# Decoder step on one core: u blocks split only where they are used, candidate sums by segments, three PSUM banks for u, and a set order of gate and u evictions

## The chip, the core and the metric

The kernel runs on one core of one Trainium2 chip. The metric is the device time of one execution in microseconds (us): the median of the runs. A change of 0.2% is about 6 us here.

## The reference, cut to what matters

One inference step of two layers, for 512 prompt tokens and 8 samples (520 tokens, padded to five tiles of 128 in places). Layer 0 mixes with gated DeltaNet and RG-LRU, layer 1 with sliding-window attention. After each mixer comes PEER, a lookup among 16384 experts:

```python
q = (tb @ w_q).reshape(PEER_BLOCK, PEER_HEADS, 2, PEER_D_SUB)
s = jnp.einsum('thcd,hcnd->thcn', q, sub_keys).astype(F32)
s_top, i_top = lax.top_k(s, PEER_TOPK)
cand = (s_top[:, :, 0, :, None] + s_top[:, :, 1, None, :]).reshape(PEER_BLOCK, PEER_HEADS, -1)
cand_idx = (i_top[:, :, 0, :, None] * PEER_N_KEYS + i_top[:, :, 1, None, :]).reshape(...)
best, pos = lax.top_k(cand, PEER_TOPK)
expert = jnp.take_along_axis(cand_idx, pos, axis=-1)
gate = jax.nn.softmax(best, axis=-1)
act = jax.nn.gelu(jnp.einsum('td,thkd->thk', tb, u_tab[expert]).astype(F32))
return jnp.einsum('thk,thkd->td', (gate * act).astype(tb.dtype), v_tab[expert])
```

## The kernel before, in words

Products of float32 operands are made of float16 halves: `split` copies a float32 tile to float16 on ACT (hi) and takes the rest on DVE (lo), and `mm3` issues three matmuls (hi with hi, hi with lo, lo with hi).

Each layer is a mixer and then `peer(layer)`. For the first 384 prompt tokens PEER is dense: the activations of all 16384 experts are computed in 128 **u blocks** of 128 experts. A u block is one load of 512 KB from `uT`, a split (`wh` on ACT, `wl` on DVE, pools of two buffers each), 24 matmuls of 384 columns into one PSUM bank (`pu`), and a gelu on ACT (`act`, L333) that reads the bank and so frees it. For the last 128 prompt tokens and the samples the experts are gathered row by row instead: POOL issues indirect DMAs (`row`, L357), DVE takes dot products with the token (L364) for u, and scaled sums (L545) for v.

The stages of `peer` are these.

- **Queries**: 16 blocks of `wq` on PE; on DVE the top 16 of each half for all tiles (`topk_half`, tiles `scs` and `swork`).
- **Pairs**: `topk_pairs` for the samples, for two halves of the gathered tile (`pairs3`) and for tile 0 (`pairs`). It adds up the candidate pairs (`cand`, L256, 16 instructions a call, one for each rank a of the first half) and their expert numbers (`ce`, L260, 33 instructions a call), takes the top 16 of 50 candidates and finds their numbers by comparisons (`eq`). Six calls are made in a layer. Meanwhile PE works on u blocks, and the gathered dot products run on DVE.
- **Gates**: for each of 3 tiles 4 parts of 32 tokens, `gates(t, part, us)`. DVE makes one-hot tiles (`oh`), PE multiplies them into `pg` (four banks), ACT copies each `pg` to `stage` (8 copies of 128x512 a part), and one DMA on ACT's queue writes the 2 MB of `stage` to `GD` in DRAM. `stage` has one buffer: the first copy of a part waits for the write of the part before. `run_u` issues u blocks between the copies.
- **Main**: for each of the 128 blocks the activations are multiplied by the gates read back, and `yps` accumulates the products with v. The u blocks that are left run here beside it. `peer` computes 79 blocks ahead of the main loop in program order, and 49 in it.

Of the PSUM's eight banks the pairs and gates stages hold two for `pu`, two for `pt` and four for `pg`.

**Blocks of u split beforehand.** At the end of each mixer `presplit` loads blocks of `uT` by halves (`pst`), splits each half in two pieces (`ppr`, on ACT and DVE), and writes the halves in float16 to DRAM (`PW`, 256 KB a write). `NPRE = (16, 12)`: 16 blocks for layer 0, 12 for layer 1. `ublock` then loads such a block (`wpr`, 512 KB) ready for PE, where any other is loaded in float32 and split.

**What sets the order.** The program is recorded, and a list scheduler that runs a timeline of its own puts the instructions of each engine in an order, across stages; on the chip each engine and each DMA queue takes them in that order. So `presplit`, written last in the mixer, is put between the mixer's own instructions, and blocks of u between those of pairs and gates.

## Time and profile before

| | us |
|---|---|
| median of 3 runs (lowest, highest) | 3012.0 (3011.1, 3014.87) |
| the profiled execution, its own time | 3010.68 |
| its span, first to last instruction | 3008.9 |
| outside the span | 1.8 |
| mean granted TensorE clock | 0.983 of 2.4 GHz |

How to read the profile: PE is TensorE's matmuls, PEld its weight loads, DVE VectorE, ACT ScalarE, POOL GpSimd, SP the engine that issues most DMAs. Times are in us from the start of the span. The view of stretches gives each engine's busy time in it, with the number of instructions in brackets, the granted clock, the busy share of the DMA engines and GB/s. The view of waits names the waiting engine and line, what released it, the total, the number of waits and the longest. Matmuls overlap in the records (one of 384 columns is shown with some 328 ns, and the next starts half of that later), so that a busy PE can still be a slow one; the number of matmuls in a stretch says how fast it went.

In this execution layer 0's mixer lies before 380, its queries end on DVE at 492, its pairs reach to 634 (the first one-hot tile), its gates to 886 (the first `yps`), its main stage to 1575. In layer 1 the same marks are 1780, 1906, 2057, 2317 and the end.

### The profile page before, as it was taken

How to read it: one execution, taken by the hardware profiler on the slowest of the kernel's cores; microseconds unless marked ns; L12 is line 12 of the kernel's file. 1: busy time of each engine (PE TensorE's matmuls, PEld its weight loads, DVE VectorE, ACT ScalarE, POOL GpSimd, SP SyncE). 2: the span in 40 equal slices, each digit the busy share in tenths (PEclk: the TensorE clock that was granted, in tenths of full speed). 3: DMA queues.
4: the chain of work that ended last, by engine and by line, in shares of the span. 5: the costliest groups of instructions: out<-in, count | busy, mean ns of one | idle time of the engine just before them, and what ended most of it. 6: DMA issues, size and time to landing. Idle time of an engine off the chain costs nothing.

```text
span 3008.9 us, 49598 instructions
## 1 busy us (share of the span) xinstructions
PE 2845.8 (95%) x18198; PEld 1726.9 (57%) x18198; DVE 2569.4 (85%) x5871; ACT 1319.3 (44%) x2171; POOL 856.1 (28%) x662
## 2 busy tenths in 40 slices
PE   8979999899999999999998899989999999999998
PEld 7768586456655555544446559645665555554443
DVE  6756789999978988889995879989987898898998
ACT  4743332356753333333335743335765333333342
POOL 2300101310024555435520000130002555454552
PEclk9999999999999999999999999999999999999999
DMA  4264424866699999999977422686569999999996
GB/s 136 72 218 149 147 86 161 295 238 217 217 339 390 366 354 363 363 358 370 352 276 246 154 79 85 211 293 213 193 216 327 390 360 360 353 359 359 362 357 234
DMA packets 332104, 798.78 MB, mean 265 GB/s; under 512 B 28611, under 2 KB 165259, under 8 KB 328020
## 3 DMA queue, kind: packets, MB, share of 16 engines
q1 hardware_dynamic: 241004, 442.78, 43.5%
q0 software_dynamic: 78336, 285.25, 25.5%
q10 hardware_dynamic: 12520, 67.58, 6.1%
q8 instruction: 142, 2.33, 0.3%
q14 instruction: 102, 0.84, 0.1%
HBM read 700.96 MB, written 93.17 MB: 264 GB/s over the span
## 4 chain that ended last, share of the span: by engine, by line
PE 66%; DVE 13%; DMA 10%; ACT 6%; issue 4%; POOL 1%; SPq 0%; ACTq 0%; DVEq 0%; POOLq 0%
PE yps L607 30%; PE pu L88 7%; PE pu L86 7%; PE pu L87 7%; DMA row<-in_u_rows,elist 2%; ACT stage L72 2%; PE pq L87 2%; DMA GD<-stage 2%; PE pq L86 2%; PE pq L88 2%; DVE wl L81 2%; DMA pst<-in_uT 2%; DVE row L364 1%; DMA PW<-ppr 1%; DMA gl<-GD 1%
## 5 line engine op out<-in xcount | busy, mean ns | idle before, releaser
L607 PE MATMUL yps<-vv,vw 128*128 128x512 f16 x4536 | 1010.8, 379 | 10.3 <-ACT vv L72 8.1
L607 PEld LDWEIGHTS <-vw 128*128 128x128 f16 x4608 | 450.4, 98 | 542.2 <-issue 17.0
L357 POOL DMA_INDIRECT row<-in_v_rows,elist x272 | 395.4, 1454 | 862.9 <-issue 251.0
L88 PE MATMUL pu<-xh,wl 128*128 128x384 f16 x1824 | 598.4, 329 | 34.2 <-DVE wl L81 33.7
L86 PE MATMUL pu<-xh,wh 128*128 128x384 f16 x1824 | 598.9, 328 | 15.6 <-ACT act L333 10.7
L87 PE MATMUL pu<-xl,wh 128*128 128x384 f16 x1824 | 598.4, 328 | 0.0
L357 POOL DMA_INDIRECT row<-in_u_rows,elist x272 | 389.1, 1430 | 679.8 <-DVE best L237 250.3
L72 ACT ACTIVATE wh<-wst 128x1024 f16<-128x1024 f32 x296 | 312.4, 1056 | 565.3 <-PE pu L87 340.3
L81 DVE SCALAR_TENSOR_TENSOR wl<-wst,wh 128x1024 f16<-128x1024 f32 x296 | 361.7, 1223 | 154.1 <-ACT wh L72 148.1
L88 PEld LDWEIGHTS <-wl 128*128 128x128 f16 x2912 | 287.4, 99 | 186.9 <-DVE wl L81 47.5
L86 PEld LDWEIGHTS <-wh 128*128 128x128 f16 x2912 | 290.1, 100 | 159.3 <-ACT wh L72 25.5
L87 PEld LDWEIGHTS <-wh 128*128 128x128 f16 x2912 | 287.6, 99 | 149.3 <-issue 14.5
L72 ACT ACTIVATE vv<-row 128x1024 f16<-128x1024 f32 x252 | 263.1, 1048 | 232.9 <-PE yps L607 182.6
L81 DVE SCALAR_TENSOR_TENSOR vv<-row,vv 128x1024 f16<-128x1024 f32 x252 | 307.6, 1221 | 49.9 <-ACT vv L72 48.1
L545 DVE SCALAR_TENSOR_TENSOR yac<-row,wgt,yac 128x1024 f32<-128x1024 f32 x268 | 343.5, 1282 | 4.5 <-DMA row<-in_v_rows,elist 2.6
L364 DVE CUSTOM_DVE_ANT_0 row<-row,xtok 128x1024 f32<-128x1024 f32 x256 | 308.4, 1220 | 20.3 <-DMA row<-in_u_rows,elist 20.1
L72 ACT ACTIVATE vw<-act 128x384 f16<-128x384 f32 x256 | 129.7, 516 | 350.8 <-PE yps L607 298.1
L72 ACT ACTIVATE stage<-pg 128x512 f32<-128x512 f32 x192 | 183.4, 1105 | 76.2 <-DMA GD<-stage 65.6
L79 DVE TENSOR_TENSOR vw<-act,vw 128x384 f16<-128x384 f32 x256 | 139.8, 553 | 24.3 <-ACT vw L72 23.6
L333 ACT ACTIVATE act<-pu 128x384 f32<-128x384 f32 x256 | 122.3, 478 | 48.4 <-PE pu L88 46.2
L87 PE MATMUL pq<-xl,wh 128*128 128x264 f16 (+1 forms) x480 | 132.9, 277 | 0.5 <-DVE xl L79 0.3
L88 PE MATMUL pq<-xh,wl 128*128 128x264 f16 (+1 forms) x480 | 132.9, 277 | 0.0
(501 smaller groups left out, 3968.4 us busy)
## 6 DMA issues: line engine op xcount, KB each, us to landing
row<-in_v_rows SPq DMA_DIRECT2D x256, 512.0 KB, 7.8
wst<-in_uT SPq DMA_DIRECT2D x228, 512.0 KB, 6.3
GD<-stage ACTq DMA_DIRECT2D x24, 2048.0 KB, 7.6
gl<-GD SPq DMA_DIRECT2D x64, 768.0 KB, 7.9
wst<-in_wq SPq DMA_DIRECT2D x32, 512.0 KB, 3.4
pst<-in_uT SPq DMA_DIRECT2D x56, 256.0 KB, 4.1
PW<-ppr SPq DMA_DIRECT2D x56, 256.0 KB, 2.9
wpr<-PW SPq DMA_DIRECT2D x28, 512.0 KB, 5.2
```

Of the source, the lines that this page charges most:

```text
L72: self.nc.scalar.activation(out, in_, AF.Copy, scale=scale)
L79: eng.tensor_sub(lo, src, hi)
L81: eng.scalar_tensor_tensor(lo, src, scale, hi, op0=OP.mult, op1=OP.subtract)
L86: mm(out, wh, xh, start=start, stop=False)
L87: mm(out, wh, xl, start=False, stop=False)
L88: mm(out, wl, xh, start=False, stop=stop)
L333: S.activation(t, ps[:, 0:ND], AF.Gelu_apprx_tanh, scale=1.0 / SCW)
L357: G.indirect_dma_start(out=r, out_offset=None, in_=src, in_offset=bass.IndirectOffsetOnAxis(ap=elist[:, k:k + 1], axis=0))
L364: V.tensor_tensor_reduce(u, u, self.xtok[:, 0] if k < P else xrep, 1.0, 0.0, OP.mult, OP.add, hd[:, k:k + 1])
L545: V.scalar_tensor_tensor(dst, vbuf.pop(n), wgt[:, k:k + 1], dst, op0=OP.mult, op1=OP.add)
L607: T.matmul(yps[t][:, o], w[:, a, c], v[:, b, o], start=x == 0 and k == 0, stop=x == P - 1 and k == 2)
```

## The change

1. `NPRE` is (0, 0): `presplit` does nothing, and every block of u is loaded in float32 and split in `peer`.
2. The sums of candidates are written by segments. Ranks that take the same range of the second half are added in one instruction with two broadcast operands: 7 instructions in place of 16 for `cand` (`CSEG`), 20 in place of 33 for `ce` (`LSEG`, whose runs of equal ranges are joined). The candidates and their order stay.
3. In the pairs and gates stages `pt` keeps one bank in place of two; the freed bank goes to `pu`, so that every third u block (u % 3 == 2) has a bank of its own pool (`third`). This holds from the first pairs to the end of the gates; ahead of them and behind them there are two banks as before.
4. In `gates` two of its three u blocks are recorded ahead of the part, the third at its middle; and the first copy to `stage` of a part is ordered on ACT behind the last ACT instruction recorded before it, the gelu of the second block (`last_on`, `behind`: an edge of order on the engine, with no semaphore).

```diff
--- before.py
+++ after.py
@@ -43,13 +43,18 @@
         for a in range(hi):
             b0, b1 = (hi - 4) // (a + 1), hi // (a + 1)
             if b1 > b0:
-                seg.append((a, b0, b1))
+                if seg and seg[-1][1:] == (a, b0, b1):
+                    seg[-1] = (seg[-1][0], a + 1, b0, b1)
+                else:
+                    seg.append((a, a + 1, b0, b1))
                 perm += [start[a] + b for b in range(b0, b1)]
         cnt.append(len(perm))
     return seg, cnt, np.array(perm, np.float32)
 
 
 LSEG, LCNT, LPERM = lookup_order()
+
+CSEG = [(a0, a1, 0, TOPK // a1) for a0, a1 in ((0, 1), (1, 2), (2, 3), (3, 4), (4, 5), (5, 8), (8, 16))]
 SCW = 1024.0
 SCV = 256.0
 SCG = 64.0
@@ -108,6 +113,18 @@
                 for q in range(0, 4, 2):
                     self.split(o[:, 0, q:q + 2], o[:, 1, q:q + 2], st[:, q:q + 2], SCW)
                 nc.sync.dma_start(self.PW[layer, b, :, :, c], o)
+
+    def behind(self, ins):
+
+        ctx = ExitStack()
+        for i in ins:
+            ctx.enter_context(self.tc.issue_after(i))
+        return ctx
+
+    def last_on(self, *engines):
+
+        ins = self.nc.cur_bb.bb.instructions
+        return [next(i for i in reversed(ins) if i.engine == e.engine) for e in engines]
 
     def ublock(self, layer, b):
         if b < self.NPRE[layer]:
@@ -250,16 +267,18 @@
         V.tensor_scalar(fx[:n, 0], fx[:n, 0], float(P), None, op0=OP.mult)
         cand = pool.tile([P, HM, NC50], F32, name="cand%d" % HM)[:, 0:H]
         ce = pool.tile([P, HM, NC50], F32, name="ce%d" % HM)[:, 0:H]
-        off = 0
-        for a in range(TOPK):
-            nb = TOPK // (a + 1)
-            V.tensor_add(cand[:n, :, off:off + nb], st[:, 0, :, a:a + 1].to_broadcast([n, H, nb]), st[:, 1, :, 0:nb])
-            off += nb
-        off = 0
-        for a, b0, b1 in LSEG:
-            V.tensor_add(ce[:n, :, off:off + b1 - b0], fx[:n, 0, :, a:a + 1].to_broadcast([n, H, b1 - b0]),
-                         fx[:n, 1, :, b0:b1])
-            off += b1 - b0
+
+        def sums(out, x, segs):
+
+            off = 0
+            for a0, a1, b0, b1 in segs:
+                s = [n, H, a1 - a0, b1 - b0]
+                o = out[:n, :, off:off + s[2] * s[3]].rearrange("p h (a b) -> p h a b", a=s[2])
+                V.tensor_add(o, x[:n, 0, :, a0:a1, None].to_broadcast(s), x[:n, 1, :, None, b0:b1].to_broadcast(s))
+                off += s[2] * s[3]
+
+        sums(cand, st, CSEG)
+        sums(ce, fx, LSEG)
         best = pool.tile([P, HM, TOPK], F32, name="best%d" % HM)[:, 0:H]
         pos = pool.tile([P, HM, TOPK], U32, name="pos%d" % HM)[:, 0:H]
         wk = pool.tile([P, NC50], F32, name="cwork")
@@ -312,6 +331,7 @@
 
         act, upair = {}, {}
         nprep, nu, live = [0], [0], [0]
+        third = []
 
         def u_prep():
             if nprep[0] < P:
@@ -324,7 +344,7 @@
                 return
             nu[0] += 1
             h, l = upair.pop(u)
-            ps = pu.tile([P, 512], F32, name="pu")
+            ps = (third[0] if third and u % 3 == 2 else pu).tile([P, 512], F32, name="pu")
             for kb in range(KB):
                 self.mm3(ps[:, 0:ND], h[:, kb], l[:, kb], self.xh[:, kb, 0:ND], self.xl[:, kb, 0:ND],
                          kb == 0, kb == KB - 1)
@@ -433,8 +453,9 @@
         TG = 32
         with tc.tile_pool(name="gates", bufs=1, reuse_waits="tile") as gp, \
                 tc.tile_pool(name="pairs", bufs=1, side="right", reuse_waits="tile") as tp, \
-                tc.tile_pool(name="topkps", bufs=2, space=bass.MemoryType.PSUM, reuse_waits="tile") as psum:
+                tc.tile_pool(name="topkps", bufs=1, space=bass.MemoryType.PSUM, reuse_waits="tile") as psum:
             lts = {}
+            third.append(psum)
 
             def pairs3(h0):
 
@@ -473,6 +494,8 @@
 
                 lt = lts[t]
                 stage = gp.tile([P, P, TG], F32, name="stage")
+                run_u(us - 1)
+                order = self.last_on(S)
                 for t4 in range(0, TG, 4):
                     if t4 % 8 == 0:
 
@@ -492,8 +515,10 @@
                         q, r = divmod(t4 % 8 + k, 2)
                         T.matmul(pg[:, k], oh[:, 0, q, :, r], oh[:, 2, q, :, r], start=True, stop=False)
                         T.matmul(pg[:, k], oh[:, 0, q, :, r], oh[:, 3, q, :, r], start=False, stop=True)
-                    self.copy(stage[:, :, t4:t4 + 4].rearrange("p i t -> p t i"), pg)
-                    if t4 * us // TG < (t4 + 4) * us // TG:
+                    with self.behind(order):
+                        self.copy(stage[:, :, t4:t4 + 4].rearrange("p i t -> p t i"), pg)
+                    order = []
+                    if t4 == TG // 2:
                         run_u(1)
                 nc.scalar.dma_start(GD[P // TG * t + part], stage)
 
@@ -527,6 +552,7 @@
                     pairs(k // 4 + 1)
                     pairs_t(k // 4 + 1)
             run_u(P)
+        third.clear()
         kctx.close()
 
 
@@ -1528,8 +1554,8 @@
             self.UP = 7
             dp = ctx.enter_context(tc.tile_pool(name="scratch", bufs=1, space=bass.MemoryType.DRAM))
             self.GD = dp.tile([12, P, P, 32], F32, name="GD")
-            self.NPRE = (16, 12)
-            self.PW = dp.tile([2, max(self.NPRE), P, 2, KB, P], F16, name="PW")
+            self.NPRE = (0, 0)
+            self.PW = dp.tile([2, max(1, *self.NPRE), P, 2, KB, P], F16, name="PW")
             self.AD = dp.tile([self.NSP, P, ND], F32, name="AD")
             self.wst = ctx.enter_context(tc.tile_pool(name="wst", bufs=3))
             self.wsp = ctx.enter_context(tc.tile_pool(name="wsp", bufs=2))
```

What the scheduler makes of it is shown at three places. **ACT, layer 0's mixer**, where the inverse of chunk matrices runs (`ia` to `ie` are its copies out of PSUM, `zth` a tanh of another projection, `ppr` the first half of a presplit). Before:

```order
L72 ACTIVATE ppr<-pst 128x256 x4
L72 ACTIVATE id<-psg_2238 128x512
L1141 ACTIVATE zth<-psp 128x256
L72 ACTIVATE ie<-psg_2252 128x512
L72 ACTIVATE ppr<-pst 128x256 x4
L72 ACTIVATE ia<-psg_2229 128x512
L72 ACTIVATE ppr<-pst 128x256 x2
L72 ACTIVATE ia<-psg_2266 128x512
```

Now, at the same place:

```order
L77 ACTIVATE ia<-psg_2218 128x512
L77 ACTIVATE id<-psg_2238 128x512
L77 ACTIVATE wh<-wst 128x1024
L1167 ACTIVATE zth<-psp 128x256
L77 ACTIVATE ia<-psg_2229 128x512
L77 ACTIVATE ie<-psg_2252 128x512
```

The pieces of `presplit` that stood between the copies of the inverse are gone; nothing was put in their place.

**DVE, layer 0's pairs**, at the last comparisons of the first `pairs3` (`row,hd` is a gathered dot product, `wl` the lower half of a u block). Before:

```order
L279 TENSOR_TENSOR eq_6136<-pf_6122,lperm 128x800
L364 ISA row,hd<-row,xrep 128x1024
L364 ISA hd 128x1
L241 MAX_INDEX pos_6291<-best_6290,cwork 128x8
L281 TENSOR_TENSOR eq_6136<-eq_6136,ce_6046 128x800
L239 MATCH_REPLACE cwork<-best_6290,cand_6239 128x50
L364 ISA row,hd<-row,xrep 128x1024
L364 ISA hd 128x1
L282 TENSOR_REDUCE ev<-eq_6136 128x4x4
```

Now:

```order
L86 SCALAR_TENSOR_TENSOR wl<-wst,wh 128x1024
L384 ISA row,hd<-row,xrep 128x1024
L384 ISA hd 128x1
L298 TENSOR_TENSOR eq_5868<-pf_5854,lperm 128x800
L256 MATCH_REPLACE cwork<-best_6012,cand_5983 128x50
L384 ISA row,hd<-row,xrep 128x1024
L384 ISA hd 128x1
L300 TENSOR_TENSOR eq_5868<-eq_5868,ce_5800 128x800
L86 SCALAR_TENSOR_TENSOR wl<-wst,wh 128x1024
```

Lower halves of u blocks now stand among the pairs from their start, where blocks split beforehand needed none. Between the last `swork` of the queries and the first one-hot tile DVE has 17 of them in layer 0 before and 32 now, and 23 and 33 in layer 1; four more stand ahead of that point, in either layer. Its sums of candidates there go from 196 to 112 instructions, and from 49 to 23 in the gates. PE has 33 whole blocks of u ahead of layer 0's first gate matmul before and 37 now, 35 and 38 in layer 1.

**ACT, layer 1's gates**, one late part, from one write of `GD` to the next. Before:

```order
L498 DMA GD<-stage 128x4096
L72 ACTIVATE wh<-wst 128x1024
L333 ACTIVATE act<-pu 128x384
L72 ACTIVATE stage<-pg 128x4x128 x4
L72 ACTIVATE wh<-wst 128x1024
L333 ACTIVATE act<-pu 128x384
L72 ACTIVATE wh<-wst 128x1024
L333 ACTIVATE act<-pu 128x384
L72 ACTIVATE stage<-pg 128x4x128 x4
L498 DMA GD<-stage 128x4096
```

Now:

```order
L523 DMA GD<-stage 128x4096
L77 ACTIVATE wh<-wst 128x1024
L353 ACTIVATE act<-pu 128x384
L77 ACTIVATE wh<-wst 128x1024
L353 ACTIVATE act<-pu 128x384
L77 ACTIVATE stage<-pg 128x4x128 x4
L77 ACTIVATE wh<-wst 128x1024
L353 ACTIVATE act<-pu 128x384
L77 ACTIVATE stage<-pg 128x4x128 x4
L523 DMA GD<-stage 128x4096
```

Two gelus in place of one stand between a write of `GD` and the copy that waits for it. Layer 0's late parts stood so already before.

## Rows read from the trace of the kernel before

**Rows 1.** The page: each engine's busy time, share of the span, instructions.

```profile
PE 2845.8 (95%) x18198; PEld 1726.9 (57%) x18198; DVE 2569.4 (85%) x5871; ACT 1319.3 (44%) x2171; POOL 856.1 (28%) x662
```

**Rows 2.** Stretches: both mixers where presplits run, then the pairs of both layers.

```profile
core 0: us, PE busy (x) PEld busy (x) DVE busy (x) ACT busy (x) POOL busy (x), PEclk, DMA share, GB/s
160.00:260.00 100.00, 84.02 (x633) 75.96 (x633) 56.88 (x131) 46.73 (x123) 0.66 (x1) 0.89 0.72 227
1600.00:1700.00 100.00, 81.41 (x650) 66.03 (x649) 69.28 (x265) 70.39 (x206) 0.00 (x0) 0.93 0.67 213
...
492.00:634.00 142.00, 123.98 (x725) 71.01 (x724) 127.52 (x553) 44.15 (x66) 49.35 (x38) 0.96 0.85 289
...
1906.00:2057.00 151.00, 131.14 (x760) 75.09 (x758) 136.81 (x572) 49.84 (x72) 50.58 (x38) 0.95 0.84 286
```

**Rows 3.** Waits between 160 and 260, layer 0's mixer.

```profile
DVE ppr L81 <- ACT ppr L72: 31.1, 19, 7.5
ACT ppr L72 <- DMA PW<-ppr: 25.1, 19, 2.9
ACT ppr L72 <- DMA pst<-in_uT: 9.3, 1, 9.3
```

**Rows 4.** Waits between 1600 and 1700, layer 1's mixer.

```profile
ACT ppr L72 <- DMA pst<-in_uT: 20.6, 9, 3.9
DVE ppr L81 <- ACT ppr L72: 16.6, 9, 3.3
```

**Rows 5.** The chain from 160 to 290 by line, as shares of that stretch.

```profile
by line: DMA PW<-ppr 24.4%; PE psg L987 11.4%; DMA pst<-in_uT 6.4%; PE psa L1191 6.1%; DMA S<-in_state_gdn 6.1%; DVE ppr L81 5.4%; ACT ppr L72 5.2%; ACT dT L1011 3.2%; issue 2.6%; PE psa L1007 2.3%; PE psp L987 2.0%; PE psa L1008 1.9%; PE p
```

**Rows 6.** The presplits' own instructions in two stretches: DVE busy, ACT busy, clock, DMA.

```profile
160.00:260.00 100.00, 24.48 (x64) 23.06 (x64) 0.89 0.72 227
1600.00:1700.00 100.00, 17.21 (x44) 15.95 (x44) 0.93 0.67 213
```

**Rows 7.** Stretches of layer 0's mixer ahead of the presplits and behind them.

```profile
100.00:140.00 40.00, 36.31 (x305) 30.72 (x303) 30.71 (x57) 32.48 (x51) 11.30 (x21) 1.00 0.21 67
260.00:300.00 40.00, 39.44 (x273) 31.64 (x271) 24.41 (x49) 13.02 (x23) 0.54 (x1) 0.98 0.29 98
```

**Rows 8.** The u blocks' instructions alone in four stretches: PE, PEld, DVE, ACT.

```profile
500.00:520.00 20.00, 19.84 (x122) 0.00 (x0) 0.00 (x0) 2.57 (x6) 1.00 0.81 269
540.00:640.00 100.00, 83.73 (x483) 0.00 (x0) 0.00 (x0) 9.79 (x21) 0.95 0.89 303
...
634.00:886.00 252.00, 203.15 (x1185) 0.00 (x0) 0.00 (x0) 23.36 (x49) 0.99 0.66 239
2057.00:2317.00 260.00, 202.40 (x1180) 0.00 (x0) 0.00 (x0) 23.58 (x49) 0.99 0.64 227
```

**Rows 9.** Groups of DVE instructions between 492 and 634, busy us and mean ns.

```profile
L81 DVE SCALAR_TENSOR_TENSOR wl<-wst,wh 128x1024 f16<-128x1024 f32 x17 | 20.7, 1215 | 1.4 <-ACT wh L72 1.4
L260 DVE TENSOR_TENSOR ce<-fx 128x8 f32<-128x8 f32 (+5 forms) x132 | 11.2, 167 | 0.0
```

**Rows 10.** DVE in order of time: start, us, instruction.

```profile
524.93 1.53 DVE L260 TENSOR_TENSOR ce<-fx 128x8 f32<-128x8 f32 x19
526.36 0.22 DVE L240 MAX8 best<-cwork 128x8 f32<-128x50 f32 x1
```

**Rows 11.** Waits between 492 and 634, layer 0's pairs.

```profile
PEld L88 <- DVE wl L81: 15.4, 9, 5.7
DVE row L364 <- DMA row<-in_u_rows,elist: 12.4, 8, 2.6
```

**Rows 12.** Waits between 640 and 880, layer 0's gates.

```profile
ACT stage L72 <- DMA GD<-stage: 25.3, 9, 4.3
```

**Rows 13.** Waits between 2080 and 2310, layer 1's gates.

```profile
ACT stage L72 <- DMA GD<-stage: 40.3, 10, 6.4
DVE wl L81 <- ACT wh L72: 32.6, 10, 4.4
```

**Rows 14.** The page: a DMA's KB and median us from issue to landing.

```profile
GD<-stage ACTq DMA_DIRECT2D x24, 2048.0 KB, 7.6
```

**Rows 15.** Waits of the whole span.

```profile
PE pu L86 <- ACT act L333: 15.7, 16, 2.7
```

## The prediction

> **What bounds the kernel now.** I read the page first: PE is busy for 95% of the span [rows 1], so time can come only from the rest, or from stretches in which a busy PE is slow. The view of stretches finds these. In layer 0's mixer from 160 to 260 and in layer 1's from 1600 to 1700, PE is idle for 16.0 and 18.6 us of 100, at a granted clock of 0.89 and 0.93 [rows 2]. In the pairs it is idle for 18.0 us of 142 and 19.9 of 151, and there DVE is busy for 127.5 and 136.8 [rows 2]: DVE sets the pace. At full pace 122 matmuls of u blocks run in 20 us, 3.93 us for a block of 24; from 540 to 640 only 483 run in 100 us, 4.97 us a block [rows 8], and PE's weight loads wait 15.4 us for `wl` [rows 11].
>
> The gates are nearly full: 252 us in layer 0 with 1185 matmuls of u, 49.4 blocks [rows 8]. These take 194 us at 3.93; 768 gate matmuls of a third of the columns take, at a third of 0.164 us, 42 (an estimate). So 16 us are lost, and by the same sum on 1180 matmuls 25 of layer 1's 260 [rows 8]. The main stages I leave out: the change issues nothing there, and the number of u blocks recorded ahead of them stays.
>
> **Presplits out of the mixers.** The waits tell what they do in an engine's order. In layer 0's stretch ACT is busy for 46.7 us and waits 25.1 for writes of `PW` and 9.3 for `pst` [rows 2, 3]: 81 us in which little else passes. DVE is busy for 56.9 and waits 31.1 for ACT's half [rows 2, 3]. The mixer's own copies stand behind these waits, and PE behind the copies. The chain agrees: writes of `PW`, loads of `pst` and both halves of the split make 41.4% of 130 us, 54 us [rows 5]. In layer 1 ACT is busy for 70.4 and waits 20.6, and DVE is busy for 69.3 and waits 16.6 [rows 2, 4]. Without the presplits' own 24.5 and 17.2 us on DVE and 23.1 and 16.0 on ACT [rows 6], both engines have half of each stretch free.
>
> What is late next is PE and the alternation of PE with a copy. The gain can't be the chain's 54 us: PE is busy for 84.0 and 81.4 us anyway [rows 2]. It lies between 0, if the alternation alone makes PE wait, and PE's idle time, 34.6 us together; a clock that recovers could add some. The nearest rows without presplits are the same mixer ahead of them and behind them, where PE is idle for 9% and 1.4% of the time [rows 7]. I take 5%: 84.0/0.95 = 88.4, a gain of 11.6, and 81.4/0.95 = 85.7, a gain of 14.3. **Together -26.** The DMAs go too, 56 loads and 56 writes in the mixers; on SP's queue the loads of states and of output weights no longer stand behind writes that wait for DVE. That is part of the same gain. The 28 loads of `wpr` become 28 loads of `wst` of the same 512 KB, at nothing: three buffers cover them as before.
>
> **The split moves into the pairs, and the sums shrink.** In layer 0's pairs DVE gets 15 more `wl` at 1.22 us [rows 9], 18.3, and one dot product that was counted in the gates, 1.2. It loses 84 of its sums. One is shown with 0.167 us [rows 9], but 19 of them pass in 1.43 us, from 524.93 to 526.36 [rows 10], 0.075 each; since the elements are still added, that is the price of an instruction, 6.3 for 84. DVE's work goes to 127.5 + 13.2 = 140.7. Its idle time, 14.5 us, is mostly the 12.4 of waiting for gathered rows [rows 11], which nothing here changes: I keep it. Four more `wl` less 22 sums stand ahead of the stretch, 4.9 - 1.7 = 3.2. So the first one-hot tile comes 16.4 us later, and PE has done four more u blocks by then, 15.7 us: +0.7 net. In layer 1, 10 more `wl` are 12.2, less 6.3, plus 3.2: 9.1 us later, and three more blocks, 11.8: -2.7. **Together -2.** ACT's 28 copies hide there: it is busy for 44 and 50 us of these stretches [rows 2].
>
> The Trainium skill ("VectorE: DVE Perf Modes", Side-by-side: where the cycles go) adds about 150 cycles of start and decoding to a DVE instruction, 0.16 us at its clock. Here 264 sums fewer (22 in each of 12 calls) would by that be worth 41 us, where 0.075 makes 20; the sum would fall by 21 us. The trace differs: these instructions start 0.075 us apart, so it decides.
>
> **Order in the gates.** A copy to `stage` that waits for the write of `GD` holds back the next `wh` behind it on ACT, then `wl` on DVE, then PE. ACT waits 25.3 us so in layer 0 and 40.3 in layer 1, where DVE waits 32.6 for `wh` [rows 12, 13]. The write lands in 7.6 us [rows 14]; two u blocks take PE 7.9, so with two gelus between, as the order now has in the late parts of both layers, the copy should find it landed. The added edge orders ACT alone and no one waits for it longer than for that second gelu; what is queued behind it, `wh` of the third block, has a block's time. I take 12 us lost a layer in place of 16 and 25: -4 and -13. The ends are 0 and all that is lost, 41. DVE loses 26 sums more in each, hidden where PE is the bound. **Together -17.**
>
> **The third bank.** PE waits 15.7 us for a gelu in the whole span, in 16 waits [rows 15], many of them of blocks that then wait for `wl`. Between 0 and -15.7; I cost it at 0, since DVE holds the pairs and two banks did for the gates of layer 0. `pt`'s lost bank costs nothing: three transposes a tile.
>
> **The sum**: -26 - 2 - 17 = -45, on the profiled execution's 3010.7: 2966. The median of the runs is 1.3 higher, so I forecast **2967**, and 2945 to 2990 with these terms.
>
> **Rivals.**
> - *The mixers are bound by their own alternation.* For it: the matmuls of the inverse wait for a copy of the product before them, and the idle 9% of rows 7 has no presplit. Against it: the chain runs through `PW` [rows 5]. With 5 us in place of 26, or with a gates term of next to nothing: 2985.
> - *Slower: DVE can't feed PE through the pairs.* `wh` and `wl` have two buffers each, so a block that comes late on DVE stops PE at once. Blocks split in the pairs now take 4.97 us in place of 3.93 [rows 8]. If the 28 blocks that came ready now lose 1.04 us each, that is +29; the pairs' late end leaves the gates 6 of their 17, and the mixers give only 10: +13, **3025**. It decides from the point where the pairs lose more than the mixers give. For it: DVE has 90% of these stretches already. Against it: the sums that go, and an order that now spreads `wl` evenly.
> - *A sum is worth its whole duration*, because dependent sums don't overlap as those of rows 10 do. 264 at 0.167 in place of 0.075 [rows 9, 10] make 24 us more, nearly all on a bound DVE: 2943. The Trainium skill's price goes this way. Against it: the pace in rows 10.
> - That the change is not what it says is ruled out by the order: no `ppr` is left, and two gelus stand ahead of the copies.
>
> **Chances.** The forecast 0.50; the mixers' or gates' gain missing 0.26; slower 0.12; the sums' whole price 0.12. Outcomes within 0.2% of 3012 (3006 to 3018), about what a measurement can tell from no change, lie between the second and the third: 0.04 of the one and 0.02 of the other. That gives faster 0.84, same 0.06, slower 0.10. For 8 in 10 the range reaches up to 3010, where both gains of the second case are missing (2967 + 26 + 17), and down to 2934, where the last case meets mixers that give all 34.6 us.
>
> **What would show it.** Right: no wait of ACT or DVE for anything of presplits, and the inverse's 100 us shortened by some 12; the queries of layer 0 starting some 12 us earlier. The pairs from the last `swork` to the first one-hot tile at about 155 us in both layers, with DVE over 90% busy. ACT's waits for `GD` under 20 us in all. Both `peer` layers alike, from first u block to first `yps` some 405 us, two u blocks further. Wrong: pairs over 165 us with PE waiting for `wl` twice as long; a mixer that is as long as before with ACT idle; or waits for `GD` that remain while the gates stay at 250 us.

## The result, and the profile after

The changed kernel takes **2977.65 us** (median of 4 runs, 2976.02 to 2983.89) against 3012.05; the ratio is 0.9893, 95% interval 0.9875 to 0.991. The forecast was 2967, the range 2934 to 3010. The profiled execution is the slowest of the four (2983.89, span 2981.8), so beside it I use the profile of a second set of runs, e0 below (span 2972.8).

The page's busy times, where [rows 1] stood:

```profile
PE 2838.3 (95%) x18198; PEld 1717.5 (58%) x18198; DVE 2545.6 (85%) x5523; ACT 1312.2 (44%) x2087; POOL 855.8 (29%) x662
```

PE is still busy for 95%: it works less long, but no denser. DVE lost 24 us and 348 instructions. The stretches of [rows 2] and [rows 8] after the change (both mixers, layer 1's as far into its stage as there, then pairs and gates of either layer; columns as there):

```profile
160.00:260.00 100.00, 98.69 (x822) 91.88 (x822) 46.92 (x95) 34.83 (x75) 1.08 (x2) 0.97 0.22 74
1588.00:1688.00 100.00, 91.99 (x812) 73.48 (x812) 67.22 (x248) 68.59 (x186) 0.00 (x0) 1.00 0.42 133
...
469.70:628.40 158.70, 136.80 (x795) 77.13 (x793) 142.15 (x500) 57.73 (x81) 50.79 (x38) 0.97 0.80 271
628.40:877.00 248.60, 239.44 (x1938) 158.18 (x1937) 221.41 (x392) 167.25 (x209) 10.60 (x8) 0.99 0.66 235
...
1879.90:2045.00 165.10, 145.54 (x819) 81.92 (x818) 143.18 (x503) 60.58 (x84) 52.05 (x38) 0.93 0.78 264
2045.00:2291.80 246.80, 236.40 (x1924) 156.92 (x1923) 219.61 (x387) 165.37 (x206) 12.10 (x8) 0.99 0.65 234
```

In the same 100 us of layer 0's mixer PE now runs 822 matmuls, not 633, and is idle for 1.3%, not 16%; the granted clock is 0.97, not 0.89. In layer 1's it runs 812, not 650, is idle for 8.0%, not 18.6%, and the clock is 1.00, not 0.93. The chain through layer 0's mixer (160 to 290) no longer names a presplit; PE's own lines head it, where [rows 5] had writes of `PW`:

```profile
by line: PE psg L1013 25.5%; DMA wst<-in_w_out_ab 6.8%; PE psa L1013 6.3%; PE psg L1019 5.2%; PE psa L1217 5.1%; DMA S<-in_state_gdn 4.2%; PE psp L93 3.8%; PE psp L91 3.8%; PE psp L92 3.8%; PE psa L1033 3.6%; DMA out_o_sgdn<-S 3.4%; PE psa 
```

The pairs went the other way. Waits in layer 0's pairs, in its gates, and in layer 1's gates, beside [rows 11 to 13]:

```profile
PEld L93 <- DVE wl L86: 25.0, 18, 3.2
DVE row L384 <- DMA row<-in_u_rows,elist: 13.5, 10, 3.8
...
DVE wl L86 <- ACT wh L77: 20.8, 9, 4.3
ACT stage L77 <- DMA GD<-stage: 16.4, 5, 3.9
...
ACT stage L77 <- DMA GD<-stage: 24.4, 7, 4.8
DVE wl L86 <- ACT wh L77: 20.4, 10, 4.3
```

PE waits for `wl` 18 times in the pairs where it waited 9 times, 25.0 us and not 15.4. In the gates ACT's waits for `GD` fell from 25.3 to 16.4 us and from 40.3 to 24.4 (17.7 and 31.9 in e0).

**One account for all runs.** Stages trade blocks of u with each other, so the length of a stage tells little. I count PE's lost time instead: a stretch's length less 3.93 us for each block of u in it, less 42 us for the gate matmuls and 497 us (a constant) for those of `yps`. Pairs run from the first u matmul to the first one-hot tile, gates to the first `yps`, main to the last. Mixers are the time to layer 0's first query matmul plus that from layer 0's last `yps` to layer 1's first query matmul. Both layers together, in us, from the profiled executions; mixers plus losses plus 2290 is the span within 1.5 us in each:

| kernel | mixers | lost in pairs | gates | main | span | ratio of medians, 95% |
|---|---|---|---|---|---|---|
| before | 606.6 | 56.4 | 41.6 | 14.4 | 3008.9 | 1 |
| changed | 562.9 | 72.4 | 33.0 | 23.1 | 2981.8 | 0.9893 (0.9875 to 0.991) |
| e0 changed, again | 561.3 | 62.7 | 35.5 | 22.5 | 2972.8 | 0.9906 (0.9877 to 0.9934) |
| e1 no presplit, rest as before | 560.2 | 55.2 | 76.2 | 21.6 | 3004.3 | 0.9994 (0.998 to 1.0009) |
| e2 presplit back | 603.9 | 56.8 | 38.3 | 17.4 | 3006.1 | 1.0008 (0.9992 to 1.0023) |
| e3 single sums | 557.8 | 66.2 | 61.3 | 33.6 | 3009.0 | 1.0008 (0.9994 to 1.0023) |
| e4 order of before | 567.2 | 68.4 | 31.6 | 21.8 | 2979.6 | 0.9892 (0.9865 to 0.9918) |
| e5 two banks | 562.2 | 55.4 | 50.4 | 27.3 | 2986.8 | 0.9969 (0.9953 to 0.9986) |
| e6 three wh, wl | 562.2 | 37.3 | 79.1 | 30.2 | 2999.2 | 0.9969 (0.9951 to 0.9986) |
| e9 presplit on POOL | 595.5 | 56.1 | 35.1 | 9.7 | 2987.0 | 0.9956 (0.994 to 0.9973) |
| e10 e6 and 40 ahead | 568.7 | 37.2 | 38.9 | 55.9 | 2991.9 | 0.9923 (0.9898 to 0.9949) |
| e11 40 ahead | 568.7 | 63.7 | 40.6 | 25.9 | 2988.6 | 0.9925 (0.9899 to 0.9951) |
| e12 presplit's DMAs alone | 579.7 | 63.8 | 34.6 | 16.0 | 2984.4 | 0.9913 (0.9887 to 0.9939) |
| e7 four row buffers | 559.2 | 52.5 | 31.3 | 22.2 | 2955.4 | 0.9859 (0.9839 to 0.988) |

So the change gave 43.7 us in the mixers and 8.6 in the gates, and took 16.0 in the pairs and 8.7 in main: -27.6, where the spans differ by -27.1. By e0 it gave 45.3 and 6.1, and took 6.3 and 8.1. Each row is one execution: the ten kernels without presplits have the same code in their mixers, but for the third buffer of e6 and e10 and what the scheduler makes of it, and take 557.8 to 568.7 us in them. So a difference of less than some 10 us between two rows is not shown by them, and whole times are judged by the ratios.

### The profile page after: what moved, and what is told of

Its sections match the earlier page's. It is cut to its first block, busy times and chain, and to the rows that moved or that the text cites. A ratio compares the mean times of both kernels' runs of the same rounds, so it can differ in the third digit from the quotient of the medians.

```text
span 2981.8 us, 49027 instructions
## 1 busy us (share of the span) xinstructions
PE 2838.3 (95%) x18198; PEld 1717.5 (58%) x18198; DVE 2545.6 (85%) x5523; ACT 1312.2 (44%) x2087; POOL 855.8 (29%) x662
## 4 chain that ended last, share of the span: by engine, by line
PE 68%; DVE 10%; DMA 8%; ACT 6%; issue 5%; POOL 1%; ACTq 0%; DVEq 0%; SPq 0%; POOLq 0%
PE yps L633 29%; PE pu L93 7%; PE pu L91 7%; PE pu L92 7%; DMA row<-in_u_rows,elist 3%; ACT stage L77 2%; PE pq L92 2%; PE pq L91 2%; PE pq L93 2%; DVE wl L86 2%; DMA GD<-stage 2%; POOL row L377 1%; PE psg L1013 1%; ACT wh L77 1%; PE psc L430 1%
## 5 line engine op out<-in xcount | busy, mean ns | idle before, releaser
L93 PE MATMUL pu<-xh,wl 128*128 128x384 f16 x2048 | 673.1, 330 | 44.4 <-DVE wl L86 43.8
L91 PE MATMUL pu<-xh,wh 128*128 128x384 f16 x2048 | 676.6, 330 | 19.6 <-ACT wh L77 18.7
L92 PE MATMUL pu<-xl,wh 128*128 128x384 f16 x2048 | 676.2, 330 | 0.0
L77 ACT ACTIVATE wh<-wst 128x1024 f16<-128x1024 f32 x324 | 342.1, 1056 | 595.9 <-PE pu L92 345.4
L86 DVE SCALAR_TENSOR_TENSOR wl<-wst,wh 128x1024 f16<-128x1024 f32 x324 | 395.5, 1223 | 155.1 <-ACT wh L77 142.0
L93 PEld LDWEIGHTS <-wl 128*128 128x128 f16 x3136 | 310.5, 99 | 219.5 <-DVE wl L86 64.0
L91 PEld LDWEIGHTS <-wh 128*128 128x128 f16 x3136 | 312.9, 100 | 188.3 <-ACT wh L77 39.8
L92 PEld LDWEIGHTS <-wh 128*128 128x128 f16 x3136 | 310.6, 99 | 156.2 <-issue 9.4
L84 DVE TENSOR_TENSOR vw<-act,vw 128x384 f16<-128x384 f32 x256 | 140.8, 555 | 36.5 <-ACT vw L77 34.6
L91 PE MATMUL pq<-xh,wh 128*128 128x264 f16 (+1 forms) x480 | 133.1, 277 | 0.0
```

Source lines behind the costliest of these rows:

```text
L77: self.nc.scalar.activation(out, in_, AF.Copy, scale=scale)
L84: eng.tensor_sub(lo, src, hi)
L86: eng.scalar_tensor_tensor(lo, src, scale, hi, op0=OP.mult, op1=OP.subtract)
L91: mm(out, wh, xh, start=start, stop=False)
L92: mm(out, wh, xl, start=False, stop=False)
L93: mm(out, wl, xh, start=False, stop=stop)
```

## The experiments

Two theories stood at first. **A**: the mixers pay, and the pairs charge about 1 us for each block that they now split. **B**: presplits cost as much where they were as where they went, and the gain is that of the sums, the bank and the order. Kernels of one set ran on one chip, each with the kernel before beside it.

### One part at a time

**e1_no_presplit**, the kernel before without presplits (the second line only sizes `PW`):

```diff
-            self.NPRE = (16, 12)
-            self.PW = dp.tile([2, max(self.NPRE), P, 2, KB, P], F16, name="PW")
+            self.NPRE = (0, 0)
+            self.PW = dp.tile([2, max(1, *self.NPRE), P, 2, KB, P], F16, name="PW")
```

> The kernel before with no blocks split beforehand and nothing else changed. Theory A (the mixers pay, the pairs charge): the first query block of layer 0 starts some 25 us earlier than 383 and layer 1's mixer takes some 18 us less than 223, 44 together, and 28 blocks more that are split in the pairs cost about 1 us each, with the long sums still there: about 2996 us. Theory B (the two sides of the presplits cancel, and the gain of the change comes from sums, bank and order): about 3012 us, within 5.

**e2_presplit_back**, the changed kernel with `NPRE` at (16, 12) again:

> The changed kernel with 16 and 12 blocks split beforehand again. Theory A: the mixers are as long as before (44 us back) and the pairs lose 28 us less: about 2994 us. Theory B: within 5 us of the changed kernel, 2973 to 2983.

Measured: 0.9994 and 1.0008. Neither half does anything alone, and together they give 1%: the parts do not add, and e2 fits neither of its two forecasts. The account shows where the time goes. Without presplits the mixers lose their 46 us in e1 as in the changed kernel, but e1's gates lose 76.2 us, not 41.6. It comes to them 6 and 4 blocks further (38.1 in both layers), and PE then runs out of blocks before the gates are ready. Waits in layer 0's gates of e1:

```profile
ACT stage L72 <- DMA GD<-stage: 39.9, 8, 7.0
...
PE yps L607 <- ACT vw L72: 12.4, 1, 12.4
```

The second row is not in the kernel before: PE stands 12.4 us at the first `yps`, with the last gates still on their way through `GD`, DVE's product and ACT's copy. In layer 1 it stands 12.6 us; the two are 25 of the 35 us that e1's gates lose more. At that point 84 blocks are done; 79 may be computed ahead, and the rest are what the scheduler can bring forward. In e2 DVE is done with the pairs sooner (127.0 and 139.9 us), but PE does fewer blocks in them (28.1 and 31.1 by the first one-hot tile, where before it did 32.2 and 33.7) and loses as much as before: DVE's saving buys nothing while blocks come ready from the mixers.

**e3_sums_single**, the changed kernel with every sum an instruction of its own:

```diff
-                if seg and seg[-1][1:] == (a, b0, b1):
-                    seg[-1] = (seg[-1][0], a + 1, b0, b1)
-                else:
-                    seg.append((a, a + 1, b0, b1))
+                seg.append((a, a + 1, b0, b1))
...
-CSEG = [(a0, a1, 0, TOPK // a1) for a0, a1 in ((0, 1), (1, 2), (2, 3), (3, 4), (4, 5), (5, 8), (8, 16))]
+CSEG = [(a0, a1, 0, TOPK // a1) for a0, a1 in ((a, a + 1) for a in range(TOPK))]
```

> The changed kernel with every sum of candidates an instruction of its own again, 264 more on DVE. If they cost their pace of 0.075 us and DVE sets the pace of the pairs: 13 to 20 us more, about 2994. If each costs its whole 0.167 us or the Trainium skill's 0.16: 40 us more, about 3018. If DVE has room for them (its 16 and 22 us of waits in the pairs take them in): under 5 us more.

Measured: 1.0008; without the sums the whole gain is gone. The page of e3:

```profile
PE 2838.1 (94%) x18198; PEld 1716.7 (57%) x18198; DVE 2561.7 (85%) x5787; ACT 1310.7 (44%) x2087; POOL 858.4 (29%) x662
```

264 instructions more keep DVE busy for 16.1 us more than in the changed kernel, 0.061 each; the span grows by 27.2 (36.2 against e0). Of that the gates lose 28.3, and in layer 1 the wait of `yps` for `vw` is back with 15.0 us. So an instruction costs what the pace of [rows 10] said, 0.075, and a little less; but at the end of the gates DVE's work and PE's blocks run out against each other, and there a late microsecond of DVE cost more than one. How much more, and by which steps, the runs do not settle. The Trainium skill ("VectorE: DVE Perf Modes", Side-by-side: where the cycles go) would make these instructions 0.16 us each by its fixed 150 cycles, an estimate of 41 us of DVE; the measured 16.1 decides against that.

**e5_two_banks**, the changed kernel with two banks for `pt` and all of u in `pu`:

```diff
-                tc.tile_pool(name="topkps", bufs=1, space=bass.MemoryType.PSUM, reuse_waits="tile") as psum:
+                tc.tile_pool(name="topkps", bufs=2, space=bass.MemoryType.PSUM, reuse_waits="tile") as psum:
...
-            third.append(psum)
```

> The changed kernel with two PSUM banks for u and two for pt again. If the third bank is worth nothing, as forecast: within 3 us of the changed kernel. If PE's waits for a gelu (15.7 us before) were what it removed: 8 to 16 us more, with these waits back in the gates.

Measured: 0.9969, so the bank is worth 0.6 to 0.8% of the time, some 20 us by the ratios, and 5 to 14 between the profiles (that of e5 is the fastest of its 12 executions). In the gates ACT's waits for `GD` and PE's waits for a gelu, layer 0 and layer 1, are:

```profile
ACT stage L77 <- DMA GD<-stage: 40.6, 10, 6.2
PE pu L91 <- ACT act L353: 6.9, 7, 3.3
...
ACT stage L77 <- DMA GD<-stage: 36.6, 9, 6.1
PE pu L91 <- ACT act L353: 5.7, 5, 3.3
```

With three banks the first are 16.4 and 24.4 (17.7 and 31.9 in e0), and of the second only one is left, of 0.8 us in layer 1 (0.9 in e0): a third block can be multiplied while ACT stands at the copy. So the waits for a gelu are 12.6 us with two banks, as the second forecast of e5 had them back; the rest of the 20 us is not traced to a wait.

**e4_gates_order_back**, the changed kernel with the u blocks spread over a part as before and no edge:

```diff
-                run_u(us - 1)
-                order = self.last_on(S)
...
-                    with self.behind(order):
-                        self.copy(stage[:, :, t4:t4 + 4].rearrange("p i t -> p t i"), pg)
-                    order = []
-                    if t4 == TG // 2:
+                    self.copy(stage[:, :, t4:t4 + 4].rearrange("p i t -> p t i"), pg)
+                    if t4 * us // TG < (t4 + 4) * us // TG:
                         run_u(1)
```

> The changed kernel with the gates' u blocks spread as before and no order between their gelus and the copies. If that order is what keeps the gates' loss at 16 us a layer: 8 to 20 us more than the changed kernel, all of it in the gates, with ACT's waits for the write of GD back at 25 to 40 us a layer. If the shorter sums do that by freeing DVE: within 4 us.

Measured: 0.9892, and the gates lose 31.6 us, where the changed kernel loses 33.0 and 35.5: no worth of the set order shows, and by the intervals it is under some 10 us. Waits for `GD` are 21.3 and 28.9 us without it, 50.2 together; with it they are 40.8 in the first profile and 49.6 in e0, so it is not shown to shorten them either.

**e0_after**, the changed kernel a second time, on the chip of e4, e6 and e9:

> The changed kernel itself, beside the kernel before on the chip of this call, as the mark for the others. 0.989 of the kernel before; mixers of about 358 and 204 us, and about 51 us of PE's time lost in each layer's pairs and gates together, if what the one profile shows holds from run to run.

Measured: 0.9906. Its pairs in layer 1 take 156.8 us where the first profile has 165.1: the pairs vary by 8 us from one execution to another.

### What in a presplit costs a mixer

**e9_presplit_pool** and **e12_dmas_alone** are the changed kernel with 16 and 12 blocks put back in the mixers: in e9 POOL splits them in three instructions (peer loads them ready), in e12 each half is loaded and written out unsplit to scratch that is never read, and `pst` gets the buffers of `ppr`. Of both edits the lines in `presplit` are shown; the others set the number of blocks and the size of `PW`.

```diff
-                    self.split(o[:, 0, q:q + 2], o[:, 1, q:q + 2], st[:, q:q + 2], SCW)
+                    x = st[:, q:q + 2]
+                    nc.gpsimd.tensor_scalar(x, x, SCW, None, op0=OP.mult)
+                    nc.gpsimd.tensor_copy(o[:, 0, q:q + 2], x)
+                    nc.gpsimd.tensor_tensor(o[:, 1, q:q + 2], x, o[:, 0, q:q + 2], op=OP.subtract)
```

> The changed kernel with 16 and 12 blocks split beforehand again, by POOL, which is idle in those stretches. If the mixers lost their time to ACT and DVE waiting in order behind the presplits: mixers stay at 358 and 204 us and the pairs and gates get back what 28 ready blocks save, 2960 to 2970. If the DMAs of the presplits (28 MB) are the cost, or POOL is too slow and the first u blocks wait for it: no better than the changed kernel, or worse.

```diff
-                st = pool.tile([P, 4, P], F32, name="pst", bufs=PB - 1 if layer == 0 else PC)
+                st = pool.tile([P, 4, P], F32, name="pst", bufs=2 * PB - 3 if layer == 0 else 2 * PC)
...
-                o = pool.tile([P, 2, 4, P], F16, name="ppr", bufs=PB - 2 if layer == 0 else PC)
-                for q in range(0, 4, 2):
-                    self.split(o[:, 0, q:q + 2], o[:, 1, q:q + 2], st[:, q:q + 2], SCW)
-                nc.sync.dma_start(self.PW[layer, b, :, :, c], o)
+                nc.sync.dma_start(self.PW[layer, b, :, :, 2 * hf:2 * hf + 2], st.rearrange("p (a b) c -> p a b c", a=2))
```

> The changed kernel with the presplits' DMAs put back in the mixers and not their splits: every half block of uT is loaded on SP's queue and written as it came to scratch that nothing reads, 56 loads and 56 writes of 256 KB as before; peer splits all its blocks itself as in the changed kernel, so the output is the reference's. Theory A (the mixers paid because ACT and DVE stand in order behind splits that wait for loads and writes): the inverse's 100 us keep PE busy for over 96 us, the mixers take 358 to 364 and 205 to 210 us, and the time is 2980 to 2992. Theory B (the DMAs themselves are the price: on SP's queue the loads of states, weights and keys stand behind them): the mixers take 370 to 383 and 213 to 224 us, and the time is 3000 to 3018.

Measured: 0.9956 and 0.9913; by the ratios e12 can't be told from the changed kernel, and fits neither theory whole (2985.8 us as in A, mixers of 367.4 and 212.3 us between the two). Mixers of e0, e12 and e2 are 561.3, 579.7 and 603.9 us: the DMAs alone cost 18.4 us, the splits on ACT and DVE 24.2 more. But e0 and e2 ran on another chip than e12; beside e10 and e11, which ran on e12's and have no presplits (568.7 both), the DMAs cost 11.0, which leaves more to the splits. The first 100 us of the inverse, of e9 and of e12:

```profile
160.00:260.00 100.00, 98.42 (x801) 92.81 (x799) 44.84 (x84) 33.71 (x72) 60.45 (x91) 0.92 0.47 151
```

```profile
160.00:260.00 100.00, 98.34 (x783) 92.34 (x784) 40.93 (x83) 33.12 (x71) 1.08 (x2) 0.90 0.74 238
```

With the splits off ACT and DVE, PE is busy there for 98% even under the presplits' DMAs (98.69 without presplits, 84.02 in [rows 2], 87.41 in e2): the idle PE of [rows 2] was the mixer's copies in order behind splits. What the DMAs cost shows in layer 1, where e12's mixer takes 212.3 us and those of the ten kernels without presplits 199.4 to 205.2. PE waits there for lower halves of the queries that a DMA on SP's queue, the queue of `pst` and `PW`, puts into `QS`; in e12, then in e0:

```profile
PE psl L1434 <- DMA QS<-ql: 9.4, 5, 3.4
```

```profile
PE psl L1437 <- DMA QS<-ql: 0.3, 1, 0.3
```

Whether it is late by its place in the queue or because the DMA engines are busy is not told apart.

In layer 0 no cost of the DMAs is shown: 367.4 us in e12, 356.2 to 366.2 in the ten. Part of that scatter is the clock. From 230 to 240 PE runs at full clock in e0 and at about half of it (1.2 GHz) in e12; but e4, which has no presplits, runs so too. The same two stretches of e0, e12 and e4:

```profile
230.00:235.00 5.00, 5.00 (x49) 4.93 (x49) 2.27 (x4) 1.48 (x3) 0.00 (x0) 1.00 0.42 141
235.00:240.00 5.00, 5.00 (x48) 5.00 (x47) 0.00 (x0) 2.01 (x4) 0.00 (x0) 1.00 0.36 120
```

```profile
230.00:235.00 5.00, 4.91 (x29) 4.16 (x28) 1.76 (x4) 0.30 (x2) 0.00 (x0) 0.59 0.67 205
235.00:240.00 5.00, 4.63 (x21) 4.63 (x22) 0.64 (x1) 0.54 (x1) 0.00 (x0) 0.50 0.22 68
```

```profile
230.00:235.00 5.00, 5.00 (x29) 4.66 (x29) 2.40 (x4) 0.60 (x1) 0.00 (x0) 0.52 0.18 56
235.00:240.00 5.00, 5.00 (x24) 5.00 (x25) 0.00 (x0) 0.93 (x2) 0.00 (x0) 0.50 0.33 107
```

PE is busy by the records in all three, and runs 97, 50 and 53 matmuls. From 225 to 230 it was as busy in e4 as in e0 (47 and 48 matmuls at 1.00), and why the clock falls in the one and not in the other is not shown. In e9 POOL pays in layer 0: the three instructions take it 0.96, 0.53 and 0.79 us a piece, 142 us for the layer, and the mixer ends no sooner than with presplits on ACT and DVE (382.7 us against 379.9 in e2). Layer 1's does (212.8 against 224.0), as e12's.

### Where the pairs' loss can be won back

**e6_three_halves**: three buffers for `wh` and `wl`, so that PE need not stop for each late half (the ring gives up one).

```diff
-            self.RING, self.NSP, self.UG, self.GU, self.ROWS = 50, 32, 3, 3, 9
+            self.RING, self.NSP, self.UG, self.GU, self.ROWS = 49, 32, 3, 3, 9
...
-            self.wsp = ctx.enter_context(tc.tile_pool(name="wsp", bufs=2))
+            self.wsp = ctx.enter_context(tc.tile_pool(name="wsp", bufs=3))
```

> The changed kernel with three buffers for the halves of a u block in place of two, and a ring of 49 activations in place of 50 to make room. If two buffers tie PE to DVE's unevenness: 10 us less lost in each layer's pairs, 15 to 20 us less in all. If DVE's mean pace sets the pairs: within 4 us.

Measured: 0.9969, slower than the changed kernel. PE's loss in the pairs halves (62.7 to 37.3) and the gates lose more than that again (35.5 to 79.1), in layer 0 at the same place as in e1:

```profile
ACT stage L77 <- DMA GD<-stage: 40.1, 9, 7.1
...
PE yps L633 <- ACT vw L77: 19.8, 1, 19.8
```

**e10_halves_ahead** (e6) and **e11_ahead** (the changed kernel) may compute 8 blocks more ahead. In e11:

```diff
-            self.RING, self.NSP, self.UG, self.GU, self.ROWS = 50, 32, 3, 3, 9
+            self.RING, self.NSP, self.UG, self.GU, self.ROWS = 50, 40, 3, 3, 9
```

> The changed kernel with three buffers for wh and wl (ring of 49) and 40 blocks of u written out in place of 32, so that 86 and not 78 can be computed ahead of the main stage; in the order 90 whole blocks stand ahead of the first yps in place of 83. With three buffers alone the pairs lost 18 us of PE in place of 35 and the gates 39.6 in place of 16.3, with a wait of yps for vw of up to 19.8 us at their end: 3001 us. Theory A (at the end of the gates PE has no block of u left, and waits for the last gates to be written, read and multiplied): the blocks that are now allowed fill that time; the pairs lose 18 to 20 us a layer as with three buffers alone, the gates under 20, the wait of yps for vw is under 3 us, and the time is 2950 to 2970, under both kernels. Theory B (DVE sets the gates' end, and each block more in the gates gives it 1.2 us of wl and ACT its wh): the gates become longer by what PE is filled with, PE loses about as much in main, which also reads 8 more blocks back: 2990 to 3005.

> The changed kernel with 40 blocks of u written out in place of 32 and nothing else; in the order 87 whole blocks stand ahead of the first yps in place of 83.5. Theory A (PE runs dry at the end of the gates only in those versions that reach it early): the changed kernel has no wait of yps for vw there and loses 16 us in each layer's gates, so there is little to fill: 2970 to 2983, gates' loss 12 to 17 us, pairs as before (158 to 165 us). Theory B: DVE sets the gates' end, so 3.5 blocks more make the gates longer by 4 to 14 us and main shorter by 14 at most, and main reads 8 blocks more: 2978 to 2995.

Measured: 0.9923 and 0.9925, no better than the changed kernel. The wait at the first `yps` is gone in e10 and its gates lose 38.9, as theory A of e10 said; but main loses 33 us more than in the changed kernel (55.9 and 23.1; why is not shown), and in e11 the gates lose 5 to 8 more. The mixers of both take 6 to 7 us more, as far as they scatter. More room to work ahead moves the loss: by the ratios it wins back some 14 us of what the three buffers cost (e10 and e6), and neither kernel beats the changed one.

**e7_four_rows**: DVE's own idle time.

```diff
-        rows = [kctx.enter_context(tc.tile_pool(name="rows", bufs=3, side="right", reuse_waits="tile"))]
+        rows = [kctx.enter_context(tc.tile_pool(name="rows", bufs=4, side="right", reuse_waits="tile"))]
```

> The changed kernel with four buffers in place of three for the gathered rows of the pairs and gates stages, and nothing else. In the profile of the changed kernel DVE waits 13.5 and 17.2 us in the two pairs stages for gathered rows, and POOL waits 35.9 us in the first of them for a dot product to free the buffer of the next gather. Theory A (DVE's own order sets the pace of the pairs, so that any time in which it stands idle there is paid in full): these waits fall to under 6 us a layer, the pairs become 6 to 12 us shorter a layer, the gates stay within 3 us, and the time is 2960 to 2973. Theory B (the pairs are set by DVE and PE in turn, wl by wl, and time won there comes back at the end of the gates, as with three buffers of wh and wl): the waits fall, but pairs and gates together stay within 5 us a layer, 2973 to 2985. Theory C (the gathers are set by the DMAs, busy for over 70% there, and not by the buffers): the waits stay over 10 us, and the time is 2975 to 2985.

Measured: 2961.37 us, 0.9859. Both pairs stages, and DVE's waits for rows in them:

```profile
469.50:619.80 150.30, 136.13 (x799) 77.90 (x798) 141.06 (x496) 58.35 (x82) 47.34 (x38) 0.97 0.81 287
1865.60:2016.50 150.90, 137.43 (x797) 78.26 (x796) 140.97 (x496) 59.01 (x82) 49.79 (x38) 0.96 0.82 286
...
DVE row L384 <- DMA row<-in_u_rows,elist: 6.2, 5, 2.7
...
DVE row L384 <- DMA row<-in_u_rows,elist: 7.1, 5, 2.2
```

DVE has the same 141 us of work and waits 7.3 and 10.1 us less; the pairs are 8.4 and 14.2 us shorter than in the first profile (7.5 and 5.9 than in e0), with as many blocks done in layer 0 and one fewer in layer 1, and the gates give nothing back (31.3). That is theory A of e7, but for waits a little above its 6 us. It beats the kernel before, and by the ratios the changed one by 10 to 14 us, though the intervals overlap.

## Why the prediction came out, step by step

**The mixers, -26 forecast, -43.7 measured.** The mechanism was right, and "I take 5%" idle nearly so: it is 1.3% in layer 0 and 8.0% in layer 1, which by the same division would give 26.4. The term was mis-sized at "a clock that recovers could add some", which went into the sum at nothing. The clock rose from 0.89 to 0.97 and from 0.93 to 1.00; PE's busy 84.0 and 81.4 us at those clocks and idle shares would take 78.1 and 82.3, a gain of 39.6 (an estimate from the two stretches), close to the 43.7. I called the SP queue "part of the same gain" and gave it no price; e12 puts the DMAs at 11 to 18 us, 7 or more of them in layer 1. The first rival, a mixer bound by its own alternation, falls.

**The pairs, -2 forecast, +16.0 measured (+6.3 in e0).** DVE came out as worked: 142.15 and 143.18 us busy for 140.7 and 142.7. One failing step is "PE has done four more u blocks by then": it has 2.9 and 2.4 more where four and three were counted, since I took the order's count at the first gate matmul for that at the first one-hot tile. That is 6.7 of the 18 us. The other is DVE's idle time, kept at 14.5 and 14.2: it was 16.6 and 21.9, but 16.1 and 14.1 in e0, so that part varies from run to run. The slower rival's mechanism was at work (PE's waits for `wl` doubled in layer 0 from 9 to 18), at 6 to 16 us rather than its 29.

**The gates, -17 forecast, -8.6 measured, for another reason.** "Order in the gates" named the order and the edge, and e4 shows no worth of them. The sums (e3) and the bank (e5) carry these stages. The step that failed is "the copy should find it landed": waits for `GD` were forecast under 20 us in all and are 40.8 (49.6 in e0). With gates of 248.6 and 246.8 us that is the prediction's own last sign of being wrong. The time from first u block to first `yps`, forecast at 405 us, is 421.7 and 426.3.

**The third bank, 0 forecast.** It is worth some 20 us by e5. The step that failed was to price it by PE's waits for a gelu in the trace of before [rows 15] and to leave that at nothing: that trace had blocks coming ready, and without them two banks make PE wait 12.6 us for a gelu in the gates alone.

**Main, left out, +8.7.** Blocks ahead of the first `yps` did not stay: 83.5 and 84.0, from 81.5 and 82.7. Why main then loses more is not shown.

**Adding the terms** was itself a step, and e1 and e2 show it to be wrong: -44 and the rest are not separate gains. As I read e1 to e3, presplits were a way of feeding PE through pairs that DVE could not feed, and they can go only since the sums freed DVE; what the runs show is that neither works without the other. That the sum came within 11 us is in part luck: -18 too little in the mixers stands against +18 in the pairs, +8 in the gates and +9 in main.

**The sums' whole price** (2943) was rejected rightly as a price of DVE (16.1 us for 264, near the prediction's 20 and far from the rival's 44). Yet losing them costs 27 to 36 us of span, between the two: the place decides, not the instruction alone.

## What to carry to other kernels

Where stages trade work with each other, account for the lost time of the busiest engine over all of them, not for stage lengths; a gain that shows up again as loss one stage later points to a bound on another engine. Here deeper buffers and more room behind the engine that sets the pace moved a loss about (e6, e10, e11), and a buffer that keeps that engine itself from waiting removed some (e7). And before a loss is put down to one part, look at the same stretch of a run without that part: e4, without presplits, has the half clock of e12. Last, parts of a change that meet on one engine have to be tried together: here each half alone measured as nothing.

## What was not expected

Presplits' DMAs, with no instruction of ACT or DVE behind them, held up a small DMA on their queue in layer 1's mixer: PE waits 9.4 us for `QS` in place of 0.3. In layer 0's mixer PE runs at half its clock for some 10 us in e4, e6, e10 and e12, and some 10 us later in e11, and not in e0, though e4 and e11 have e0's code there: e4, e6, e10 and e11 take 361.4 to 366.2 us, the other six without presplits 356.2 to 358.9. And one buffer more for rows shortened DVE's waits by 11.3 us against e0 (13.7 and 10.9 to 6.2 and 7.1) and PE's loss in the pairs by 10.2: there a microsecond of DVE's idle time was worth about a microsecond. The span fell by 17.4; the rest lies in gates and mixers, within what they vary.
